# A transformer block in float32: the MLP's first product as a 2x2 block product in seven multiplications

## The chip, the core and the metric

The kernel runs on one core of one Trainium2 chip. The metric is the time on the device of one execution in microseconds, as the median of several runs. The shape is fixed: 512 tokens, model width 1024, an MLP of 4096 hidden columns, all in float32.

## The reference, cut to what matters

The block mixes the tokens (a gated linear attention and a latent attention, merged by gates), projects the result back, and applies an MLP with a squared ReLU between two norms:

```python
h = x
h = h + merged @ w_out            # merged: the token mixing, 512 x 1024
m = rmsnorm(h, g_mlp)             # 512 x 1024
h = h + square(relu(m @ w_ff1)) @ w_ff2     # w_ff1: 1024 x 4096, w_ff2: 4096 x 1024
out = rmsnorm(h, g_final)
```

The result has to be of float32 precision. The change concerns the line with `w_ff1` and `w_ff2`, and the end of the line before it, beside which the MLP begins.

## The kernel before

**Precision.** TensorE multiplies a rounded float32 type. So every operand is split into a high part (a rounded copy, ScalarE, L93) and a low part (the rest, `src - hi`, VectorE, L94), and one product is three matmuls (`mm3`, L88 to L90: high by high, high by low, low by high). Whatever is multiplied has to go through a split first. `halves` is a pool of four pairs of high and low tiles for weights.

**The MLP before.** The hidden columns are done in four quarters (`qd`) of 1024. Each quarter has two parts, called f and g after their tiles.
In f, `hidden` forms 128 hidden columns for all tokens (`proj_begin` loads and splits the weights, `proj_run` multiplies): 8 steps over the model width, three matmuls each, 512 tokens wide, accumulated in the PSUM bank `f`. There are eight such products a quarter. `pair_units` takes the ReLU and the square (ScalarE) and makes the seven left operands that g needs: `left_sums` adds and subtracts the token halves and column halves (VectorE), and `split_first`, `split_sum` and `split_corner` split them.
In g, the quarter's hidden tile (512 x 1024) is multiplied with 1024 rows of `w_ff2` as a 2x2 block product by a scheme with seven multiplications instead of eight. Blocks are 256 tokens by 512 columns on the left and 512 by 512 on the right. The weight blocks are called B11, B12, B21, B22, and B11 is overwritten by sums and differences of them (`add_w2`, VectorE, L1000, 1024 elements wide). `ORDER` gives the sequence of the seven: 1, 5, 6, 3, 7, 4, 2. One multiplication (`block_product`) is 24 matmuls, 512 wide, for each of two row blocks. Its weights are made ready two products ahead (`prep`). The results are gathered in PSUM (`gx`, `gz`, `gw`) and added to the residual rows by `add_rows` (L1488, VectorE).

**The part before the MLP.** The product with `w_out` runs in seven multiplications as well (`wo_product`). `flipped` transposes the normed rows, two blocks of 128 tokens at a time for each token half, and `Flipped.evacuate` scales and splits the transposed rows from PSUM into `mT`, the operand of all f products. The first two f products (`early`) are begun beside the end of the product with `w_out`.

**What sets the order.** The code lists the operations, and a scheduler then orders them on each engine by estimated times, except where an order is written out: `in_program_order` fixes the order of the code on TensorE, VectorE and ScalarE up to the beginning of quarter 0, and on GpSimd up to there too; `goes_behind` moves single operations on named engines. Each engine takes its own instructions strictly in order and waits at each for its operands. Plain loads are issued by SyncE (SP); transfers that add to the tile they land in are issued by GpSimd. `stage` is a pool of three tiles (tag `wf`) for weights that are loaded. [...]

## Time and profile before

| | |
|---|---|
| median of 3 runs | 751.37 us (750.8 to 751.4) |
| span of the profiled execution | 749.5 us |
| TensorE busy | 740.9 us, 3698 matmuls |
| VectorE busy | 589.9 us, 853 operations |
| ScalarE busy | 461.8 us, 789 operations |
| GpSimd busy | 173.3 us, 244 operations |
| moved to and from the chip's memory | 83.25 MB read, 2.10 MB written |

The profile is one execution, taken on the core by the hardware profiler. PE is TensorE, PEld its weight load, DVE VectorE, ACT ScalarE, POOL GpSimd, SP SyncE. A row of the trace has the start in us, the duration, the engine, the line of the code, the operation, the tiles written and read, and the shapes; a bracket at its end tells how long the engine had been idle and what it waited for. The chain of waits follows the work that ended last back from the last instruction, and shares the span out by engine. The MLP takes from about 412 us to the end: quarter 0 to 512, then a quarter each 82 us, and the last one up to 749.

### The profile page before, as it was taken

The numbers are of one execution on the slowest core, as the hardware profiler recorded it, in microseconds if no ns is written. First come the engines' busy times: TensorE is split into PE (matmuls) and PEld (weight loads), VectorE is DVE, ScalarE is ACT, GpSimd is POOL, SyncE is SP. The second block draws the span as 40 slices with busy tenths as digits, with TensorE's granted clock in tenths as the row PEclk, the third lists the DMA queues.
The fourth block names the chain that finished last, engine by engine and source line by source line (L and its number), as shares of the span: only waits on it lengthen the run. The fifth ranks groups of instructions, "written<-read, shape, count | busy, mean of one in ns | idle before, by whom it ended". The sixth has DMA issues, their size and how long they took to land.

```text
span 749.5 us, 10256 instructions
## 1 busy us (share of the span) xinstructions
PE 740.9 (99%) x3698; PEld 628.1 (84%) x3698; DVE 589.9 (79%) x853; ACT 461.8 (62%) x789; POOL 173.3 (23%) x244
## 2 busy tenths in 40 slices
PE   9999999999999999999999999999999999999996
PEld 7888888888889888899988988888888888888885
DVE  7777887989988787888898788857697578747785
ACT  7556574686686576887956765436643464445644
POOL 0732010252663732256741100000000000000023
PEclk9999999999999999999999999999999999999999
DMA  9849682611321234459797410551136310640003
GB/s 311 265 113 228 193 176 84 103 40 29 84 57 33 46 89 106 110 143 254 196 240 230 121 56 28 169 172 53 57 101 182 112 57 27 196 143 0 29 0 113
DMA packets 94723, 88.90 MB, mean 119 GB/s; under 512 B 15793, under 2 KB 66993, under 8 KB 94673
## 3 DMA queue, kind: packets, MB, share of 16 engines
q1 hardware_dynamic: 88176, 75.64, 34.1%
q0 software_dynamic: 6208, 12.32, 9.3%
q8 instruction: 29, 0.48, 0.3%
q10 hardware_dynamic: 288, 0.28, 0.1%
q14 instruction: 22, 0.17, 0.1%
HBM read 83.25 MB, written 2.10 MB: 114 GB/s over the span
## 4 chain that ended last, share of the span: by engine, by line
PE 98%; issue 0%; DVE 0%; POOL 0%; ACT 0%; POOLq 0%
PE f L89 8%; PE f L88 8%; PE f L90 8%; PE gx L88 4%; PE gx L89 4%; PE gx L90 4%; PE first L330 3%; PE gz L88 2%; PE gz L89 2%; PE tp L1145 2%; PE gz L90 2%; PE zb L88 1%; PE zb L89 1%; PE zb L90 1%; PE av L89 1%; PE av L90 1%
## 5 line engine op out<-in xcount | busy, mean ns | idle before, releaser
L1750 POOL DMA_DIRECT2D gfin<-in_g_final x1 | 0.6, 629 | 283.4 <-PE f L90 283.4
L1000 DVE TENSOR_TENSOR w<-w,w 128x1024 f32<-128x1024 f32 x32 | 38.8, 1222 | 0.3
L1125 DVE TENSOR_REDUCE top<-s 128x1 f32<-128x512 f32 x32 | 21.6, 683 | 4.9 <-PE s L90 4.8
L1130 ACT ACTIVATE e<-s,top 128x512 f32<-128x512 f32 x32 | 22.0, 687 | 3.5 <-DVE top L1125 2.5
L94 DVE TENSOR_TENSOR pT<-tp,pT 128x512 fp32r<-128x512 f32 x32 | 21.8, 683 | 2.4 <-ACT pT L93 2.0
L1488 DVE TENSOR_TENSOR h<-h,gx 128x512 f32<-128x512 f32 x32 | 21.5, 683 | 1.9 <-PE gx L90 1.8
L93 ACT ACTIVATE pT<-tp 128x512 fp32r<-128x512 f32 x32 | 19.0, 595 | 3.2 <-PE tp L1145 3.2
L1145 PE MATMUL tp<-ident,e 128*128 128x128 f32 x128 | 19.4, 274 | 0.0
L88 PE MATMUL av<-pT,v 128*128 128x256 f32 x64 | 19.1, 299 | 0.0
L93 ACT ACTIVATE ghb<-y 128x512 fp32r<-128x512 f32 x16 | 10.1, 633 | 14.0 <-DVE y L946 14.0
L1554 ACT ACTIVATE fa<-f 128x512 f32<-128x512 f32 x32 | 18.5, 579 | 0.0
L90 PE MATMUL av<-pT,v 128*128 128x256 f32 x64 | 18.2, 285 | 0.0
L89 PE MATMUL av<-pT,v 128*128 128x256 f32 x64 | 18.2, 284 | 0.0
L1145 PEld LDWEIGHTS tp<-ident,e 128*128 128x128 f32 x128 | 15.2, 140 | 3.1 <-ACT e L1136 0.7
L94 POOL TENSOR_TENSOR qF<-qk,qF 128x512 fp32r<-128x512 f32 x4 | 6.6, 1642 | 37.6 <-ACT qF L93 37.6
L93 ACT ACTIVATE b_00h<-w 128x1024 fp32r<-128x1024 f32 x7 | 7.4, 1060 | 12.6 <-PE gx L90 6.0
L93 ACT ACTIVATE b_10h<-w 128x1024 fp32r<-128x1024 f32 x7 | 7.4, 1059 | 12.1 <-PE gz L90 6.0
L93 ACT ACTIVATE b_20h<-w 128x1024 fp32r<-128x1024 f32 x7 | 7.4, 1059 | 12.1 <-PE gz L90 6.0
L88 PE MATMUL s<-kbuf,q 96*128 96x512 f32 x32 | 14.1, 439 | 0.0
L1563 ACT ACTIVATE px<-fa 128x256 f32<-128x256 f32 x32 | 13.4, 418 | 1.0
L671 POOL DMA_DIRECT2D gvw<-in_w_in x4 | 4.8, 1226 | 38.7 <-DVE gvw L676 34.0
L996 POOL DMA_DIRECT2D w<-in_w_out x10 | 12.3, 1402 | 6.5 <-DVE bo60l L94 5.3
(1802 smaller groups left out, 2950.5 us busy)
## 6 DMA issues: line engine op xcount, KB each, us to landing
w<-in_w_ff SPq DMA_DIRECT2D x64, 256.0 KB, 3.6
w<-in_w_out POOLq DMA_DIRECT2D x10, 512.0 KB, 8.5
grw<-in_w_in SPq DMA_DIRECT2D x8, 512.0 KB, 9.3
zaw<-in_w_in SPq DMA_DIRECT2D x8, 512.0 KB, 8.0
gvw<-in_w_in SPq DMA_DIRECT2D x8, 512.0 KB, 4.9
w<-in_w_out SPq DMA_DIRECT2D x16, 256.0 KB, 5.6
x<-in_xt SPq DMA_DIRECT2D x8, 256.0 KB, 5.1
vw<-in_w_first SPq DMA_DIRECT2D x8, 256.0 KB, 5.3
```

The lines of the kernel that those rows point to most:

```text
L88: nc.tensor.matmul(acc, lh, rh, start=start, stop=False, skip_group_check=onto)
L89: nc.tensor.matmul(acc, lh, rl, start=False, stop=False, skip_group_check=onto)
L90: nc.tensor.matmul(acc, ll, rh, start=False, stop=stop, skip_group_check=onto)
L93: nc.scalar.activation(hi, src, AF.Copy)
L94: rest.tensor_tensor(lo, src, raw(hi), op=ALU.subtract)
L330: nc.tensor.matmul(f_accs[i], a[:, i * P : (i + 1) * P], b, start=k == 0 and x == 0, stop=k == KD - 1 and x == 2)
L1000: nc.vector.tensor_tensor(wq[dst][g], wq[x][g], wq[y][g], op=op)
L1125: nc.vector.tensor_reduce(top, acc, axis=AX.X, op=ALU.max, negate=True)
L1130: nc.scalar.activation(e, acc, AF.Exp, bias=top, accum_out=tot[:, qt % 2 : qt % 2 + 1])
L1145: nc.tensor.transpose(tp[:, k * P : (k + 1) * P], e[:, k * P : (k + 1) * P], ident)
L1488: nc.vector.tensor_tensor(hc, hc, acc, op=op)
L1554: nc.scalar.activation(a, acc, AF.Relu)
```

## The change

The f part of each quarter is multiplied by seven as well. The left operand is the normed input `m` in blocks of 256 tokens by 512 columns, and the right one is a 1024 x 1024 piece of `w_ff1` in blocks of 512. So one f product is now 48 matmuls, all 256 tokens wide, and there are seven a quarter instead of eight of 24 that are 512 wide.

- The left operands of f are the same for all quarters and are made once, in quarter 0, from the transposed rows in PSUM (`m_upper`, `m_lower`, `m_sum`, `m_split`). The sums of the upper half (`m_upper_raw`) and two of the others are made on GpSimd. `mT` and `Flipped.evacuate` are gone (`fm.block` hands out the bank instead).
- A class `Mlp` holds one part (f or g) of one quarter, and `phases` lists the eight in turn. The sequence of products is `SEVEN` = 1, 2, 5, 6, 3, 7, 4, and `ORDER` = 1, 5, 6, 3, 7, 4, 2 for the last g.
- Weights: a part loads its blocks with `load` (SP), and forms the sums in place. Behind the split for product 1, GpSimd adds B12 to B11 (two operations of 1024) and issues a transfer that adds B22 onto B12 (`onto`). Before product 6, VectorE adds B22 to B11, and behind it GpSimd issues a transfer that adds B21 onto B11.
- `keep` moves the results of f out of PSUM, `left_sums` forms g's left operands in place: one difference on VectorE, the other three sums (six operations of 512) on GpSimd, where before all were on VectorE. `split_left` splits them, and those of products 6, 3 and 7 only at the beginning of g.
- Every part prepares its weights two products ahead, across the border between parts. The order of the code is held on TensorE, VectorE and ScalarE through the first products of quarter 0.

The diff, cut (where removed lines are left out, the functions above show them):

```diff
...
+        def block(self, half, k):
+            c = (k // 4) * 256
+            return self.banks[half][k % 4][:, c : c + 256], self.gains[:, k : k + 1]
...
-    def add_w2(dst, x, y, op):
-        for g in range(NP // 2):
-            nc.vector.tensor_tensor(wq[dst][g], wq[x][g], wq[y][g], op=op)
...
+    m_left, m_raw = {}, {}
+    def m_upper():
+        for m in (1, 2):
+            m_left[m] = quarter(f"mh{m}"), quarter(f"ml{m}")
+        for k in range(KD):
+            hi, lo = m_left[1 + k // NP]
+            src, gain = fm.block(0, k)
+            split_scaled(hi[:, k % NP], lo[:, k % NP], src, gain)
+    def m_upper_raw():
+        for m in (1, 2):
+            hi, lo = m_left[m]
+            m_raw[m] = pair_tiles(f"mr{m}")
+            for b, dst in enumerate(m_raw[m]):
+                c = slice(2 * b, 2 * b + 2)
+                nc.gpsimd.tensor_tensor(dst, raw(hi[:, c]), raw(lo[:, c]), op=ALU.add)
+    def m_split(m):
+        m_left[m] = hi, lo = quarter(f"mh{m}"), quarter(f"ml{m}")
+        for b, s in enumerate(m_raw[m]):
+            c = slice(2 * b, 2 * b + 2)
+            split(hi[:, c], lo[:, c], s)
+    def m_lower():
+        a22, s1 = pair_tiles("mr4"), pair_tiles("mr5")
+        m_raw[4], m_raw[5] = a22, s1
+        for b in range(2):
+            for i in range(2):
+                src, gain = fm.block(1, NP + 2 * b + i)
+                nc.scalar.activation(a22[b][:, i], src, AF.Copy, scale=gain)
+                src, gain = fm.block(1, 2 * b + i)
+                nc.vector.scalar_tensor_tensor(s1[b][:, i], src, gain, a22[b][:, i], op0=ALU.mult, op1=ALU.subtract)
+        m_split(5)
+    def m_lower_raw():
+        m_raw[0] = a21 = pair_tiles("mr0")
+        for k in range(NP):
+            src, gain = fm.block(1, k)
+            nc.scalar.activation(a21[k // 2][:, k % 2], src, AF.Copy, scale=gain)
+    def m_sum(m, x, y, op, eng=nc.gpsimd):
+        m_raw[m] = pair_tiles(f"mr{m}")
+        for dst, a, b in zip(m_raw[m], m_raw[x], m_raw[y]):
+            eng.tensor_tensor(dst, a, b, op=op)
...
+    class Mlp:
+        def __init__(self, n):
+            self.n, self.qd, self.second = n, n // 2, n % 2 == 1
+            self.name = f"{'g' if self.second else 'f'}{self.qd}"
+            self.order = ORDER if n == 2 * NQ - 1 else SEVEN
+            self.right, self.left, self.accs = {}, {}, {}
+        def source(self, x, g):
+            w, r, c = (w2, self.qd * D, 0) if self.second else (w1, 0, self.qd * D)
+            r += (x // 2) * S + g * 2 * P
+            c += (x % 2) * S
+            return w[r : r + 2 * P, c : c + S].rearrange("(k p) w -> p k w", p=P)
+        def tiles(self, x):
+            if x == B22:
+                if x not in ring:
+                    ring[x] = [stage(2, S, f"w22{g}") for g in range(2)]
+                return ring[x]
+            return wq[{B11: B21 if self.second else B11, B21: B22, B12: B12}[x]]
+        def load(self, x):
+            for g, dst in enumerate(self.tiles(x)):
+                nc.sync.dma_start(dst, self.source(x, g))
+        def onto(self, dst, x):
+            for g, d in enumerate(self.tiles(dst)):
+                nc.gpsimd.dma_start(d, self.source(x, g), accum_op=ALU.add)
+        def add(self, dst, x, eng, gs=range(2)):
+            for g in gs:
+                a, b = self.tiles(dst)[g], self.tiles(x)[g]
+                eng.tensor_tensor(a, a, b, op=ALU.add)
+        def split_right(self, m, g, late=False):
+            wh, wl = halves(2, S, f"{self.name}{m}{g}")
+            src = self.tiles({2: B21, 3: B22, 7: B12}.get(m, B11))[g]
+            nc.scalar.activation(wh, src, AF.Copy)
+            self.right.setdefault(m, []).append((wh, wl))
+            def lows():
+                nc.vector.tensor_tensor(wl, src, raw(wh), op=ALU.subtract)
+            return lows if late else lows()
+        def behind(self, m):
+            after_ = phases[self.n + 1 : self.n + 3]
+            if m == 1:
+                self.add(B11, B12, nc.gpsimd)
+                self.onto(B12, B22)
+            elif m == 6:
+                self.onto(B11, B21)
+            elif m == 4:
+                if len(after_) == 2:
+                    after_[1].load(B11)
+            elif m in (2, 3, 7) and after_:
+                after_[0].load({2: B21, 3: B22, 7: B12}[m])
+        def prepare(self, m):
+            if m == 6:
+                self.add(B11, B22, nc.vector)
+            for g in range(2):
+                self.split_right(m, g)
+            self.behind(m)
+        def banks(self, m):
+            if m in (1, 2, 5):
+                tag = {1: "at" if self.second else "mm", 2: "mm", 5: "at"}[m]
+                self.accs[m] = [ps(tag, f"{self.name}{'xwz'[m // 2]}{b}") for b in range(2)]
+            return self.accs[{2: 2, 5: 5, 3: 5}.get(m, 1)]
+        def first(self, m, by_rows=False):
+            accs = self.banks(m)
+            right = self.right.pop(m)
+            lh, ll = m_left[m]
+            steps_ = [(b, i, p) for b in range(2) for i in range(2) for p in range(NP)]
+            if by_rows:
+                steps_.sort(key=lambda x: x[2])
+            for b, i, p in steps_:
+                wh, wl = right[p // 2]
+                c = slice((2 * b + i) * P, (2 * b + i + 1) * P)
+                mm3(accs[b][:, i * HT : (i + 1) * HT], wh[:, p % 2, c], wl[:, p % 2, c], lh[:, p], ll[:, p],
+                    m in (1, 2, 5) and p == 0 and i == 0, p == NP - 1, True)
+        def keep(self, m):
+            accs = self.accs[{2: 2, 5: 5, 3: 5}.get(m, 1)]
+            c = {1: 1, 2: 1, 5: 4, 6: 2, 3: 2, 7: 4, 4: 0}[m]
+            if m in (1, 5, 6, 4):
+                self.left[c] = pair_tiles(f"{self.name}a{c}")
+            for d, acc in zip(self.left[c], accs):
+                acc = acc.rearrange("p (a b) -> p a b", a=2)
+                if m in (1, 5, 6):
+                    nc.scalar.activation(d, acc, AF.Copy, scale=-1.0 if m == 6 else 1.0)
+                    continue
+                if m == 4:
+                    nc.scalar.activation(d, acc, AF.Relu)
+                else:
+                    nc.vector.tensor_tensor(d, d, acc, op=ALU.subtract if m == 7 else ALU.add)
+                    nc.scalar.activation(d, d, AF.Relu)
+                nc.scalar.activation(d, d, AF.Square)
+            if m in (2, 3, 7):
+                self.split_left(c)
+        def split_left(self, m, lows=None):
+            highs = pair_tiles(f"{self.name}h{m}", F32R)
+            lows = lows or pair_tiles(f"{self.name}l{m}", F32R)
+            for s, hi, lo in zip(self.left[m], highs, lows):
+                split(hi, lo, s)
+            self.left[m, "hl"] = highs, lows
+        def left_sums(self):
+            a11, a12, a21, a22 = (self.left[x] for x in (1, 2, 0, 4))
+            def sums(eng, dst, a, b, op):
+                for d, x, y in zip(dst, a, b):
+                    eng.tensor_tensor(d, x, y, op=op)
+            sums(nc.vector, a22, a21, a22, ALU.subtract)
+            low = tl([P, 2, 2, HT], F32R, "wf", 3, f"{self.name}l5")
+            self.left[5] = a22
+            self.split_left(5, [low[:, b] for b in range(2)])
+            sums(nc.gpsimd, a21, a11, a21, ALU.subtract)
+            sums(nc.gpsimd, a11, a22, a11, ALU.subtract)
+            sums(nc.gpsimd, a12, a12, a11, ALU.add)
+            self.left[6], self.left[3], self.left[7] = a11, a12, a21
+        def second_product(self, m, accs, begin, rb, cols=slice(0, S), out_cols=slice(0, S)):
+            highs, lows = phases[self.n - 1].left[m, "hl"]
+            for p in range(NP):
+                c = slice(rb * P, (rb + 1) * P)
+                lh, ll = (x[p // 2][:, p % 2, c] for x in (highs, lows))
+                wh, wl = self.right[m][p // 2]
+                mm3(accs[rb][:, out_cols], lh, ll, wh[:, p % 2, cols], wl[:, p % 2, cols],
+                    begin and p == 0, p == NP - 1, not begin)
...
+    phases = []
+    phases += [Mlp(n) for n in range(2 * NQ)]
+    f0 = phases[0]
...
-    load_w2(0, B21)
+    phases[1].load(B11)
     flipped(0)
-    at = traced()
-    early = [proj_begin(w1, 0, "f00", "mm")]
-    goes_behind((at, traced()), span["sums"], SP_ONLY)
+    f0.split_right(1, 0)
     first_half_square(2, 1)
...
-    fm.evacuate(0)
+    m_upper()
     first_half_square(3, 1)
...
+    f0.add(B11, B12, nc.gpsimd, (0,))
+    lows = f0.split_right(1, 1, True)
     wo_product(4, (0,))
     add_rows(2, 0, xs_[0])
     second_half_square(2, 0)
     wo_product(4, (1,))
-    at = traced()
     add_rows(3, 0, xs_[1])
     rs2 = row_rstd(hparts[2])
     second_half_square(3, 0)
...
     rs3 = row_rstd(hparts[3])
     scaled(2, rs2)
     scaled(3, rs3)
-    span["norm", 3] = at, traced()
-    proj_run(early[0], mT, 0)
-    proj_run(early[1], mT, 0, range(5))
+    for g in range(2):
+        f0.split_right(2, g)
+    f0.behind(2)
+    f0.add(B11, B12, nc.vector, (1,))
+    m_upper_raw()
+    f0.onto(B12, B22)
+    f0.first(1, True)
     flipped(2)
     flipped(3)
...
+    f0.first(2)
+    m_lower()
+    f0.split_right(5, 0)
+    m_sum(6, 5, 1, ALU.subtract, nc.vector)
+    m_lower_raw()
+    f0.split_right(5, 1)
+    m_split(6)
+    m_sum(7, 1, 0, ALU.subtract)
+    m_sum(3, 2, 6, ALU.add)
+    f0.keep(1)
+    f0.prepare(6)
+    f0.first(5, True)
+    f0.keep(2)
+    f0.keep(5)
+    m_split(3)
+    f0.prepare(3)
+    f0.first(6)
     in_program_order(begun, PE_ONLY + SPLITTERS)
     in_program_order(attending, (mybir.EngineType.Pool,))
...
+    f0.prepare(7)
+    f0.keep(6)
+    m_split(7)
+    m_split(4)
+    steps = [(ph, m) for ph in phases for m in ph.order]
+    for n, (ph, m) in enumerate(steps):
+        if n < 4:
+            continue
+        last = ph is phases[-1]
+        ahead, behind = None, False
+        if n + 2 < len(steps):
+            ahead = steps[n + 2]
+            behind = last and ahead[1] == 2
+            if not behind:
+                ahead[0].prepare(ahead[1])
+        if not ph.second:
+            ph.first(m)
+            ph.keep(m)
+            if m == 4:
+                ph.left_sums()
+            continue
+        f_ph = phases[ph.n - 1]
+        at = ph.order.index(m)
+        if last and at == 0:
             gfin = u4("gfin", F32, (P, D))
             nc.gpsimd.dma_start(gfin, t["g_final"].partition_broadcast(P))
...
+        if at < 3:
+            f_ph.split_left((6, 3, 7)[at])
+        if m == 4 and last:
+            last_rows(ph, ph.banks(4))
+            break
+        accs = ph.banks(m)
+        adding = traced()
+        for rb in range(2):
+            ph.second_product(m, accs, m in (1, 2, 5), rb)
+            upper, lower = rb, 2 + rb
+            if m in (1, 2):
+                add_rows(upper, 0, accs[rb])
+            elif m in (6, 3):
+                add_rows(upper, 1, accs[rb], ALU.subtract if m == 6 else ALU.add)
+            elif m in (5, 7):
+                add_rows(lower, 1, accs[rb], ALU.subtract if m == 7 else ALU.add)
             else:
...
+                add_rows(lower, 0, accs[rb])
+            if last and m in (3, 7):
+                out_first(upper if m == 3 else lower)
+        if behind:
+            added = traced()
+            ahead[0].prepare(ahead[1])
+            goes_behind((added, traced()), (adding, added), SPLITTERS[1:])
...
```

178 lines of the change are left out of this document (24 added, 154 removed).

## Prediction

> **What bounds the kernel now.** I read the totals and the chain of waits on the page first, then the matmuls in order of time, then the stretches of the MLP.
>
> ```profile
> span 749.5 us, 10256 instructions
> PE 740.9 (99%) x3698; PEld 628.1 (84%) x3698; DVE 589.9 (79%) x853; ACT 461.8 (62%) x789; POOL 173.3 (23%) x244
> PE 98%; issue 0%; DVE 0%; POOL 0%; ACT 0%; POOLq 0%
> 461.00:512.00 51.00, 51.00 (x225) 42.22 (x226) 36.23 (x46) 21.98 (x28) 0.00 (x0) 1.00 0.47 139
> 699.48 0.63 POOL L1750 DMA_DIRECT2D gfin<-in_g_final  x1 [283.40 <-PE f L90]
> ```
>
> TensorE carries 98% of the chain and is busy 99% of the span; every other engine has room. The fourth line is one stretch of the MLP (columns: time, then busy us of TensorE, weight load, VectorE, ScalarE, GpSimd, granted clock, DMA share, GB/s): VectorE 36 of 51 us, GpSimd nothing. The last row says that GpSimd rests 283 us before it, so through the MLP. A saving of TensorE time is therefore a saving of the whole, for as long as the other engines hand over in time. The times of the runs have a median of 751.4 us; the span of the profiled execution is 749.5, so about 1.9 us lie around it. I sum against the span and add 1.9.
>
> **The matmuls.** The price of both widths stands in the trace, in the same place and with a new stationary operand each time.
>
> ```profile
> 412.13 0.28 PE L88 MATMUL f<-mT,f00h 128*128 128x256 f32 x1
> 415.00 0.28 PE L88 MATMUL f<-mT,f01h 128*128 128x256 f32 x1
> ...
> 430.88 0.39 PE L88 MATMUL f<-mT,f03h 128*128 128x512 f32 x1
> 452.64 0.39 PE L88 MATMUL f<-mT,f07h 128*128 128x512 f32 x1
> ```
>
> The first two rows are 24 matmuls apart, 2.87 us: 0.1196 us for 256 tokens. The other two are 96 apart, 21.76 us: 0.2267 for 512. Before, the first product is 96 narrow and 720 wide matmuls: 11.5 + 163.2 = 174.7 us. After it is 4 quarters of 7 products of 48 narrow ones, 1344 x 0.1196 = 160.7. The second product keeps its 672 wide ones. TensorE saves 14.0 us, 3.3 to 3.5 a quarter. [...]
>
> One f product now takes 48 x 0.1196 = 5.74 us, one g product 24 x 0.2267 = 5.44.
>
> **What the other engines get.** Durations from start to start:
>
> ```profile
> 710.10 1.22 DVE L94 TENSOR_TENSOR b_30l<-w,b_30h 128x1024 fp32r<-128x1024 f32 x1
> 711.24 0.69 DVE L94 TENSOR_TENSOR glc<-z,ghc 128x512 fp32r<-128x512 f32 x1
> 711.84 1.22 DVE L94 TENSOR_TENSOR b_31l<-w,b_31h 128x1024 fp32r<-128x1024 f32 x1
> ...
> 404.01 1.05 ACT L93 ACTIVATE bo40h<-w 128x1024 fp32r<-128x1024 f32 x1
> 404.96 1.04 ACT L93 ACTIVATE bo41h<-w 128x1024 fp32r<-128x1024 f32 x1
> ...
> 591.41 0.62 ACT L93 ACTIVATE ga<-px 128x512 fp32r<-128x512 f32 x1
> 591.93 0.41 ACT L93 ACTIVATE gd<-qx 128x256 fp32r<-128x256 f32 x1
> 593.27 0.63 ACT L93 ACTIVATE ghb<-y 128x512 fp32r<-128x512 f32 x1 [0.94 <-DVE y L946]
> ```
>
> VectorE: 1.14 us for 1024 wide, 0.60 for 512. ScalarE: 0.95, and 0.52 to 0.63 for 512. A quarter now has on VectorE 28 splits and 4 weight sums of 1024 (36.5 us) and 36 operations of 512 (21.6): 58 of the 78.3 us that TensorE would need. ScalarE has 28 copies and some 36 operations of 512, about 47. Neither is a bound by its total. The weights become 16 plain transfers of 512 KB and 8 accumulating ones, 12 MB, 153 GB/s over 78.3 us, about what the quoted stretch moves at a DMA share of 0.47.
>
> GpSimd gets four weight sums of 1024 and six left sums of 512 a quarter. Its price, and what it does to VectorE:
>
> ```profile
> 34.57 0.75 POOL L638 TENSOR_TENSOR xz<-x 128x256 f32<-128x256 f32 x1
> 35.03 1.37 DVE L94 TENSOR_TENSOR gr10l<-grw,gr10h 128x1024 fp32r<-128x1024 f32 x1 [1.08 <-ACT gr10h L93]
> 35.28 1.72 POOL L639 TENSOR_TENSOR xz<-x,xy 128x256 f32<-128x256 f32 x1
> 36.33 1.75 DVE L94 TENSOR_TENSOR gr11l<-grw,gr11h 128x1024 fp32r<-128x1024 f32 x1
> 36.96 1.72 POOL L638 TENSOR_TENSOR xz<-x 128x256 f32<-128x256 f32 x1
> ...
> 727.17 1.29 POOL L1591 TENSOR_TENSOR ms<-h,gfin 128x512 f32<-128x512 f32 x1
> 727.55 1.99 DVE L94 TENSOR_TENSOR b_31l<-w,b_31h 128x1024 fp32r<-128x1024 f32 x1
> 733.63 1.21 DVE L94 TENSOR_TENSOR b_31l<-w,b_31h 128x1024 fp32r<-128x1024 f32 x1
> 733.84 2.16 POOL L1591 TENSOR_TENSOR ms<-h,gfin 128x512 f32<-128x512 f32 x1
> 734.76 0.68 DVE L1488 TENSOR_TENSOR h<-h,gx 128x512 f32<-128x512 f32 x1
> ...
> 136.04 2.44 POOL L671 DMA_DIRECT2D gvw<-in_w_in  x2 [34.02 <-DVE gvw L676]
> 136.71 1.22 DVE L94 TENSOR_TENSOR gv50l<-gvw,gv50h 128x1024 fp32r<-128x1024 f32 x1
> ```
>
> A GpSimd sum of 256 takes 0.75 us alone, of 512 1.29; 1024 is not shown. It lies between 1.29 (no dearer than 512) and 3.4 (twice the longest row here at 256, 1.72); the step of 0.54 per 256 gives 2.4, which I take. Where two operations on SBUF meet, the later one waits for the earlier: at 727.55 VectorE takes 1.99 in place of 1.22, at 733.84 GpSimd 2.16 in place of 1.29, and from 34.57 to 38.6 they go strictly in turn. An operation that reads PSUM (734.76) is not held, and issuing a transfer (136.04, 1.2 us each) holds nobody. So sums moved to GpSimd take VectorE's time for operations on SBUF all the same, and at 1.29 for 0.60. [...]
>
> **Where it lies on the path.** The f stages have slack: their two GpSimd sums precede product 5, with product 2 (5.74 us) between. The change from f to g has none. Let T be the end of f's product 4 in quarter 2, so g's products 1, 2, 5, 6 should start at T, T+5.44, T+10.88, T+16.32. The split buffers of g's product 1 come free with f's product 7, at T-5.74; behind them stand one sum from PSUM (0.60) and the first split (1.14), so the first GpSimd weight sum can start at T-3.9. In the changed kernel's order, what must then be done up to the second weight split of g's product 6 is, on VectorE, 9 operations of 1024 (the other splits of products 1, 2, 5, 6 and the two sums with B22) and 9 of 512 on SBUF: 10.3 + 5.4 = 15.7 us. On GpSimd it is both weight sums and all six left sums, because ScalarE's queue has the left splits that wait for those sums ahead of the weight copy: 4.8 + 7.7 = 12.5. In turn that is 28.2 us, to T+24.3. TensorE wants this tile at its eighth matmul of product 6, T+16.32+1.6 = T+17.9. It waits 6.4 us, part of it already in product 5. Quarter 1 has one 512 more: 7.0. Quarter 3: 6.4. Quarter 4 goes 1, 5, 6, so product 6 comes at T+10.88, and it needs both halves of its left sums: VectorE 12.8, GpSimd 11.3, to T+20.2, wanted at T+12.7: 7.5. Together 27.3 us. The floor of these terms is nothing (no operations meet), the ceiling with 3.4 us for a sum of 1024 is 8 x 1.0 more.
>
> Quarter 1 also has a head that is issued in written order. Between the first matmul of product 6 and that of product 3 stand f061's low split (1.14), a PSUM sum (0.60), ten ScalarE operations of 512 (5.5), a weight copy (0.95) and its low split (1.14): 9.4 us against 5.74. That is 3.7 late, whatever GpSimd does.
>
> ```profile
> 414.03 2.05 POOL L184 TENSOR_TENSOR hp<-hp,mhalf 128x1 f32<-128x1 f32 x2 [1.88 <-DVE hp L181]
> ...
> 417.00 1.75 PE mb L199 x16
> ...
> w<-in_w_out POOLq DMA_DIRECT2D x10, 512.0 KB, 8.5
> ```
>
> The first row is two small powers that hold GpSimd until 416.1. Then its eight sums of 512 (10.3) stand against VectorE's 8 operations of 1024 and 6 of 512 on SBUF (12.7) until product 6 has its low split: to 439.1. Product 6 should begin at 412.1 + 3 x 5.74 + 1.75 for the transposes (second row) = 431.1, so up to 8.0 more. The head costs 3.7 to 11.7; only two of the eight sums are needed early, so I take the middle, 7.7.
>
> Sum: 749.5 - 14.0 + 27.3 + 7.7 = 770.5 span, 772.4 us as timed. Accumulating transfers (third row: 8.5 us from issue to landing at 512 KB) have three products of cover and I cost them at nothing; without it, see the third rival.
>
> **Rivals.**
> First, faster: the sums meet VectorE in its idle time. For it speaks VectorE's idle share of a quarter, 20 of 78 us, and that GpSimd is idle in the MLP now; against it that the 28.2 us above must fit between T-3.9 and T+17.9, 21.8 us. It decides if less than about 6 us of GpSimd's 12.5 collide. Then only the head's 3.7 and about 2 at the last change are left: 751.4 - 14.0 + 5.7 = 743.
>
> Second, half of the collisions are hidden and the head costs its floor: 751.4 - 14.0 + 13.6 + 3.7 = 755. For it: product 5's wait and product 6's overlap with PSUM operations that are not held. Against: they are already left out of my count.
>
> Third, the transfer onto B11 is late too. In g it is issued only after product 6's splits, T+24.3; two issues and 8.5 us later, T+35.2, product 4's copy may begin, and product 4 starts at T+32.6+6.4 = T+39.0. Copy and two low splits take 3.2 us, so 0.6 us is spare; 3 us more of landing would cost about 2.4 a quarter: 782. The 8.5 speaks against it, being a median under load.
>
> **Chances.** Mine 0.62 (own range 762 to 782), the first rival 0.21, the second 0.09, the third 0.08. The range goes from 741 to 782. What this kernel's runs can tell from no change is about 0.2%, 1.5 us. Faster 0.22 (first rival and a little of the second), same 0.02, slower 0.76.
>
> **What would show it.** Each step right: narrow matmuls 0.12 us apart; in g's products 5 and 6 TensorE idle 6 to 7 us a quarter, released by VectorE's low splits; GpSimd left sums above 1.29 us and VectorE splits above 1.22 between T-4 and T+24; f stages of quarters 2 to 4 at 40.2 us without idle time; a gap of 3 to 4 us before f0's product 3. The prediction is wrong if GpSimd's left sums run at 1.29 while VectorE's splits keep 1.22, if narrow matmuls in long runs are dearer than 0.12, or if TensorE waits for something not in this list, such as PSUM banks or a transfer.

## The result and the profile after

The changed kernel takes 788.05 us (786.5 to 788.6), the kernel before beside it 751.38: a ratio of 1.0487, 95% interval 1.0472 to 1.0502. The forecast was slower, 772 us, in a range of 741 to 782; the direction is right and the time is 6 us outside the range. One execution of a later run (both edits together, below), the one that was profiled, took 2290 us where the other three took 772 to 775, and is left out of that run's time.

From the page of the changed kernel: the span, the busy times, the granted clock in 40 slices, and the chain of waits by engine. The last line is the clock row of the kernel before.

```profile
span 786.6 us, 11492 instructions
PE 746.1 (95%) x4226; PEld 650.0 (83%) x4226; DVE 664.6 (84%) x830; ACT 496.3 (63%) x807; POOL 309.3 (39%) x323
PEclk9999999999999999999999899999989999999898
PE 72%; DVE 18%; issue 6%; ACT 3%; POOL 1%; DVEq 0%; POOLq 0%; ACTq 0%
...
PEclk9999999999999999999999999999999999999999
```

TensorE has 528 more matmuls and is busy 5 us longer, though it should have saved 14. The clock row shows part of why: 9 in all slices before, it is 8 in four slices of the MLP now. The chain that was 98% TensorE has 18% on VectorE.

The same kernel by stages: f of quarter 1 (with the transposes), g of quarter 1, f and g of quarter 2, g of quarter 4 to the end. Columns: time, busy us of TensorE, weight load, VectorE, ScalarE, GpSimd, then granted clock, DMA share, GB/s.

```profile
412.50:469.20 56.70, 47.32 (x354) 45.46 (x353) 48.99 (x51) 38.19 (x63) 26.32 (x17) 0.94 0.46 112
469.20:515.80 46.60, 41.02 (x171) 32.30 (x170) 44.39 (x43) 22.10 (x28) 22.18 (x14) 0.96 0.53 136
515.80:556.10 40.30, 40.30 (x337) 40.30 (x336) 30.18 (x28) 28.03 (x40) 9.14 (x6) 1.00 0.65 157
556.10:602.80 46.70, 42.30 (x170) 32.88 (x169) 44.38 (x42) 20.11 (x25) 21.85 (x14) 0.93 0.54 135
730.20:786.60 56.40, 41.99 (x181) 33.19 (x180) 46.02 (x50) 25.67 (x44) 29.69 (x23) 0.90 0.33 75
```

By matmuls and transposes alone these stages should take 41.9, 38.1, 40.2, 38.1 and (as before) 45.7 us. The f stage of quarter 2 is there, with no idle time. Every g is 8.5 us or more over, and quarter 1's f 14.8. In the g stages of quarters 1 to 3 VectorE is busy 44.4 of some 46.7 us, the time included for which GpSimd holds it up; in quarter 4, which has the end of the kernel in it, 46.0 of 56.4.

What TensorE waited for, the longest first (total us, times, longest):

```profile
PE g3z L90 <- DVE f3l L94: 4.3, 2, 3.3
PE f0z L90 <- DVE f051l L1586: 2.5, 1, 2.5
PE g0z L89 <- DVE g051l L1586: 2.5, 1, 2.5
PE g2z L89 <- DVE g250l L1586: 2.1, 1, 2.1
PE g1z L89 <- DVE g150l L1586: 2.1, 1, 2.1
PE g3x L88 <- DVE h L1465: 1.8, 1, 1.8
...
PE g1z L88 <- DVE h L1465: 0.8, 1, 0.8
```

The largest are of the kind that the prediction names, for low splits in g's product 5 and in the head. Another kind it doesn't name: VectorE's read (`h`, L1465) of an earlier product in the same PSUM banks, 0.8 to 1.0 us before g's product 3 in quarters 1 to 3, and 1.8 us before product 6 in quarter 4.

The change from f to g in quarter 2, on VectorE, GpSimd and ScalarE (by matmuls alone g would start product 5 at 567.0):

```profile
552.46 3.31 POOL L1577 TENSOR_TENSOR w<-w,w 128x1024 f32<-128x1024 f32 x1 [20.32 <-DVE g110l L1586]
553.42 6.83 DVE L94 TENSOR_TENSOR f1l<-f1a,f1h 128x512 fp32r<-128x512 f32 x2
556.84 2.85 POOL L1577 TENSOR_TENSOR w<-w,w 128x1024 f32<-128x1024 f32 x1
560.77 1.21 DVE L1586 TENSOR_TENSOR g120l<-w,g120h 128x1024 fp32r<-128x1024 f32 x1
561.00 6.06 POOL L1664 TENSOR_TENSOR f1a<-f1a,f1a 128x512 f32<-128x512 f32 x3
561.91 2.31 DVE L1586 TENSOR_TENSOR g121l<-w,g121h 128x1024 fp32r<-128x1024 f32 x1
564.14 1.78 DVE L94 TENSOR_TENSOR f1l<-f1a,f1h 128x512 fp32r<-128x512 f32 x1
565.84 1.77 DVE L1664 TENSOR_TENSOR f1a<-f1a,f1a 128x512 f32<-128x512 f32 x1
567.65 0.64 ACT L93 ACTIVATE f1h<-f1a 128x512 fp32r<-128x512 f32 x1 [5.61 <-DVE f1a L1664]
567.76 5.18 POOL L1664 TENSOR_TENSOR f1a<-f1a,f1a 128x512 f32<-128x512 f32 x3 [0.69 <-DVE f1a L1664]
568.19 1.04 ACT L1582 ACTIVATE g150h<-w 128x1024 fp32r<-128x1024 f32 x1
569.51 2.29 DVE L1586 TENSOR_TENSOR g150l<-w,g150h 128x1024 fp32r<-128x1024 f32 x1
```

GpSimd's weight sum takes 3.31 us against VectorE's splits, and two VectorE operations of 512 take 6.83 together in place of 1.3. The three left sums behind 561.00 take 2 us each, and in turn with them g121l needs 2.31 and the left splits 1.77. That holds back the second left difference (565.84), the ScalarE split that needs it (567.65, which had ScalarE idle for 5.6 us), and with it the weight copy for product 5 in the same queue (568.19) and its low split (569.51).

Behind the wait stands a second loss. TensorE's matmuls there:

```profile
568.03 0.39 PE L90 MATMUL g1w<-g121h,f1l 128*128 128x512 f32 x1
569.28 0.51 PE L88 MATMUL g1z<-g150h,f1h 128*128 128x512 f32 x1 [0.86 <-ACT g150h L1582]
571.85 0.79 PE L89 MATMUL g1z<-g150l,f1h 128*128 128x512 f32 x1 [2.07 <-DVE g150l L1586]
572.45 0.63 PE L90 MATMUL g1z<-g150h,f1l 128*128 128x512 f32 x1
572.87 0.63 PE L88 MATMUL g1z<-g150h,f1h 128*128 128x512 f32 x1
...
577.40 0.44 PE L89 MATMUL g1z<-g150l,f1h 128*128 128x512 f32 x1
577.67 0.40 PE L90 MATMUL g1z<-g150h,f1l 128*128 128x512 f32 x1
```

Product 5 waits 0.86 us, gets one matmul, and waits 2.07. The next 12 distances, up to 577.4, are 0.42 to 0.60 us (nine of them 0.42 or 0.43) in place of 0.2267. For each stage I took the starts of neighbouring matmuls in order of time and counted what a distance exceeds 0.1196 or 0.2267 us: excesses over 0.45 us as waits, smaller ones over 0.05 as half speed.

| stage | waits, us | half speed, us | forecast waits, us |
|---|---|---|---|
| f, quarter 1 | 10.8 | 3.9 | 7.7 |
| g, quarter 1 | 6.3 | 2.1 | 7.0 |
| g, quarter 2 | 5.1 | 3.4 | 6.4 |
| g, quarter 3 | 6.5 | 2.0 | 6.4 |
| g, quarter 4 | 8.2 | 2.8 | 7.5 |
| sum | 36.9 | 14.1 | 35.0 |

Saved 14.0, lost 36.9 + 14.1: 37.0 us. The spans differ by 37.1.

### The profile page after: what moved, and what is told of

It reads as the page before. It is cut to its first block, busy times and chain, and to the rows that moved or that the text cites. A ratio compares the mean times of both kernels' runs of the same rounds, so it can differ in the third digit from the quotient of the medians.

```text
span 786.6 us, 11492 instructions
## 1 busy us (share of the span) xinstructions
PE 746.1 (95%) x4226; PEld 650.0 (83%) x4226; DVE 664.6 (84%) x830; ACT 496.3 (63%) x807; POOL 309.3 (39%) x323
## 4 chain that ended last, share of the span: by engine, by line
PE 72%; DVE 18%; issue 6%; ACT 3%; POOL 1%; DVEq 0%; POOLq 0%; ACTq 0%
PE first L326 3%; DVE h L1465 2%; PE tp L1122 2%; DVE w L1577 2%; PE zb L88 1%; PE zb L90 1%; PE zb L89 1%; DVE f0l L94 1%; DVE f1l L94 1%; DVE f2l L94 1%; PE av L89 1%; PE av L88 1%; PE av L90 1%; DVE f3l L94 1%; PE s L88 1%
## 5 line engine op out<-in xcount | busy, mean ns | idle before, releaser
L1577 POOL TENSOR_TENSOR w<-w,w 128x1024 f32<-128x1024 f32 x15 | 41.9, 2793 | 131.2 <-DVE g010l L1586 22.3
L1572 POOL DMA_DIRECT2D w<-in_w_ff x32 | 38.8, 1224 | 59.1 <-DVE f260l L1586 10.1
L94 DVE TENSOR_TENSOR f2l<-f2a,f2h 128x512 fp32r<-128x512 f32 x14 | 17.7, 1276 | 3.0 <-ACT f2h L93 2.8
L94 DVE TENSOR_TENSOR f1l<-f1a,f1h 128x512 fp32r<-128x512 f32 x14 | 17.7, 1276 | 3.0 <-ACT f1h L93 2.8
L94 DVE TENSOR_TENSOR f3l<-f3a,f3h 128x512 fp32r<-128x512 f32 x14 | 17.1, 1230 | 2.8 <-ACT f3h L93 2.8
L90 PE MATMUL av<-pT,v 128*128 128x256 f32 x64 | 18.2, 284 | 0.0
L667 POOL DMA_DIRECT2D zaw<-in_w_in x4 | 4.8, 1215 | 32.7 <-DVE zaw L672 28.0
L94 DVE TENSOR_TENSOR f0l<-f0a,f0h 128x512 fp32r<-128x512 f32 x14 | 13.1, 950 | 3.7 <-ACT f0h L93 3.7
L1153 POOL TENSOR_TENSOR mx<-tb,yg 128x256 f32<-128x256 f32 x8 | 7.7, 967 | 19.8 <-DVE tb L1150 13.8
L93 ACT ACTIVATE f0h<-f0a 128x512 fp32r<-128x512 f32 x14 | 8.5, 620 | 9.2 <-POOL f0a L1664 6.8
L88 PE MATMUL s<-kbuf,q 96*128 96x512 f32 x32 | 14.1, 439 | 0.0
```

Of the source, the lines that this page charges most:

```text
L88: nc.tensor.matmul(acc, lh, rh, start=start, stop=False, skip_group_check=onto)
L90: nc.tensor.matmul(acc, ll, rh, start=False, stop=stop, skip_group_check=onto)
L93: nc.scalar.activation(hi, src, AF.Copy)
L94: rest.tensor_tensor(lo, src, raw(hi), op=ALU.subtract)
L1572: nc.gpsimd.dma_start(d, self.source(x, g), accum_op=ALU.add)
L1577: eng.tensor_tensor(a, a, b, op=ALU.add)
```

## The experiments

Two theories at first. In turn: VectorE's operations on SBUF and GpSimd's sums go one after the other (the split g121l above took 2.31 us in place of 1.21), and TensorE pays for it twice, by the wait and by half speed (0.42 to 0.60 us a matmul in place of 0.2267). Queue order: it is the places in VectorE's and ScalarE's queues that make product 5 late, whatever GpSimd does. All times are medians, ratios are against the kernel before on the same chip.

### Taking the sums off GpSimd

Left sums to VectorE (778.9 us, 1.0374, 1.0358 to 1.0389):

```diff
-            sums(nc.gpsimd, a21, a11, a21, ALU.subtract)
+            sums(nc.vector, a21, a11, a21, ALU.subtract)
...
```

> The six left sums of each quarter go back from GpSimd to VectorE; the weight sums stay on GpSimd. In-turn theory (VectorE's operations on SBUF and GpSimd's sums exclude each other, and TensorE loses twice, by the wait and by half speed behind it): GpSimd's 7.7 us leave the change from f to g and VectorE gets 3.6, so the waits shrink by 4 us a quarter and most of the 2 to 3 us at half speed go with them: g stages of 46.7 become about 40.5, total 760 to 770 us. Queue-order theory (what delays product 5 is the place of the second a22 difference behind weight splits in VectorE's and ScalarE's queues, GpSimd's speed is beside the point): VectorE has 3.6 us more and nothing is gained, 788 to 800.

B11 + B12 to VectorE (775.1 us, 1.0319, 1.0304 to 1.0335):

```diff
-                self.add(B11, B12, nc.gpsimd)
+                self.add(B11, B12, nc.vector)
```

> The sums B11 + B12 of all stages behind f0 go from GpSimd to VectorE; the left sums stay on GpSimd. In-turn theory: 4.8 us of GpSimd against 2.3 of VectorE, the waits in g shrink by about 2.5 us and a little of the half speed goes: 3 to 4 us a quarter, 770 to 778 us in all; the f stages stay at 40.3. Queue-order theory: 786 to 797.

B11 + B12 by an accumulating transfer (775.7 us, 1.0344, 1.0321 to 1.0367):

```diff
-                self.add(B11, B12, nc.gpsimd)
+                self.onto(B11, B12)
```

> The sums B11 + B12 of all stages behind f0 are made by an accumulating transfer in place of two GpSimd operations; GpSimd issues 2 more transfers a stage, the left sums stay on GpSimd. In-turn theory: 4.8 us leave the change from f to g and nothing comes to VectorE, the waits in g shrink from about 5.3 to 1 or 2 us and the half speed goes: 6 to 7 us a quarter, 758 to 766 us, if the transfers (6 us from issue to landing in this kernel) land in time, as 2 x 1.2 + 6 us after product 1's splits they should. Transfer theory (the sums by transfer land later than GpSimd's did, and product 5 waits for them): waits for a transfer in product 5 of f and g, 785 to 800. Queue-order theory: 786 to 790.

The first and the third edit together (773.0 us, 1.0301, 1.0280 to 1.0322). Its stages can't be read from its profile.

> Both edits: B11 + B12 by transfer, left sums on VectorE; GpSimd does no sums behind quarter 1's head. In-turn theory: on VectorE 19 us are left for 21.8, so only the 1 us before product 3 stays in each g: g stages 39 to 40 us, total 752 to 760 us; what is left over the old kernel is the head, 14.7 us against the 14.0 that TensorE saves. Queue-order theory: 788 to 800. If it comes below 751 the head must have moved too.

Each gains, 9, 13, 12 and 15 us, where the queue-order theory expected nothing. But only the second came where the in-turn theory put it, the others 9 to 13 us above their ranges, and two edits that gain 9 and 12 us alone gain 15 together.

Moving an operation to another engine also lets the scheduler order the queues anew, and in the first two runs VectorE's and ScalarE's orders did change. In the run with transfers they did not: TensorE's matmuls stand in the order of the changed kernel to the end, VectorE's and ScalarE's operations up to the last change from f to g. There quarter 2's g fell from 46.7 to 42.3 us with the two weight sums gone from GpSimd and nothing else reordered, so GpSimd's sums cost time in one and the same order, and the queue-order theory alone falls. Quarter 2's g in that run:

```profile
552.50:594.90 42.40, 39.39 (x171) 31.31 (x170) 37.89 (x40) 20.03 (x25) 17.98 (x12) 1.00 0.72 175
```

What is left there? ScalarE's weight copies,

```profile
562.75 1.06 ACT L1582 ACTIVATE g151h<-w 128x1024 fp32r<-128x1024 f32 x1 [1.01 <-DMA w<-in_w_ff]
...
569.11 1.06 ACT L1582 ACTIVATE g160h<-w 128x1024 fp32r<-128x1024 f32 x1 [4.25 <-DVE w L1577]
```

wait 1.0 us for the transfer (g151h) and 4.25 us for VectorE's sum B11 + B22 (g160h), which stands in VectorE's queue behind all of product 5's splits. So a second cause is left, the order of that queue or the amount of work in it; the order could be tried.

### The head, and the speed behind a wait

On top of both edits, the head's eight sums to VectorE as well, each where it is needed (770.5 us, 1.0246, 1.0213 to 1.0279):

```diff
-                nc.gpsimd.tensor_tensor(dst, raw(hi[:, c]), raw(lo[:, c]), op=ALU.add)
+                nc.vector.tensor_tensor(dst, raw(hi[:, c]), raw(lo[:, c]), op=ALU.add)
...
-    def m_sum(m, x, y, op, eng=nc.gpsimd):
+    def m_sum(m, x, y, op, eng=nc.vector):
...
+    m_upper_raw(1)
     m_sum(6, 5, 1, ALU.subtract, nc.vector)
...
     f0.prepare(6)
+    m_upper_raw(2)
+    m_sum(3, 2, 6, ALU.add)
```

> The kernel with B11 + B12 by transfer and the left sums on VectorE, and in quarter 1's head the eight sums of 512 moved from GpSimd to VectorE too, each where its result is first needed (two ahead of product 6's left operand, the others behind product 6's weights). In-turn theory: VectorE reaches the low splits of product 5 at about 430 us and of product 6 at 433.5 in place of 433 and 440, the head's waits shrink from 10.8 us to 4 or 5 and its half speed from 3.9 to at most 2: quarter 1's f in 47 to 50 us in place of 56.7, 8 us less than the run with both edits alone (774), so 763 to 768. Queue-order theory: VectorE has 4.8 us more to do in the head, no gain, 773 to 780. What the g stages still wait for will be seen in this trace: for a split that stands behind others in VectorE's queue (order), or for a transfer (landing).

Quarter 1's f fell from 56.7 to 53.0 us, not to 47 to 50. Products 5 and 6 were as early as expected (waits of 2.9 us in all up to there), but 3.8 us were now lost before product 3, the place and size that the prediction gives for ScalarE's written order "whatever GpSimd does"; in the changed kernel itself only 2.0 us of it show, where product 6 is later.

The speed by itself: trains of 60 matmuls with waits of chosen length between them.

```diff
+        for i in range(TRAIN):
+            nc.tensor.matmul(acc, left, src, start=i == 0, stop=i == TRAIN - 1)
+        nc.scalar.activation(keep, acc, AF.Copy)
+        for _ in range(copies):
+            nc.scalar.activation(keep, keep, AF.Copy)
+        nc.scalar.activation(right[(n + 1) % 2], keep, AF.Copy, scale=1.0 / 700)
```

> A kernel of its own that computes nothing of the reference: 45 trains of 60 matmuls (512 wide, about 13.6 us), and between two trains a wait on a chain of 2 to 10 ScalarE operations of 512, so about 1 to 5.5 us. If it is the single wait that sets the speed behind it: trains behind waits under about 2 us keep 0.227 us a matmul, those behind waits over 3.5 us begin at 0.43 for 3 to 6 us, and between the two it depends on the moment. If half speed in the changed kernel came from something else (transfers, GpSimd), no train here runs at 0.43 whatever its wait.

One row is a train: start, duration, and in brackets the wait before it.

```profile
22.58 13.89 PE L43 MATMUL acc<-right,left 128*128 128x512 f32 x60 [1.35 <-ACT right L47]
39.20 13.90 PE L43 MATMUL acc<-right,left 128*128 128x512 f32 x60 [2.74 <-ACT right L47]
118.87 15.51 PE L43 MATMUL acc<-right,left 128*128 128x512 f32 x60 [2.07 <-ACT right L47]
214.52 15.51 PE L43 MATMUL acc<-right,left 128*128 128x512 f32 x60 [2.73 <-ACT right L47]
137.77 16.50 PE L43 MATMUL acc<-right,left 128*128 128x512 f32 x60 [3.39 <-ACT right L47]
234.08 16.15 PE L43 MATMUL acc<-right,left 128*128 128x512 f32 x60 [4.05 <-ACT right L47]
```

A train takes 13.89 us at full speed. Behind waits of 1.35 to 1.41 us it always does. Behind 2.07 us it always takes 1.6 us more. Behind 2.73 or 2.74 us it once lost nothing (39.20) and 1.6 us every other time; longer waits cost 1.4 to 2.6, with no order by length. The clock that was granted shows why (columns: time, then busy us of TensorE, weight load, ScalarE, GpSimd, granted clock, DMA share, GB/s):

```profile
116.00:119.41 3.41, 1.34 (x6) 0.83 (x5) 1.85 (x3) 0.00 (x0) 1.00 0.00 0
119.41:122.82 3.41, 3.41 (x9) 2.63 (x8) 0.00 (x0) 0.00 (x0) 0.50 0.00 0
```

In this trace the clock changes only on a beat of 3.41 us, and behind a wait it stays at half for one or two beats; in the changed kernel's trace the stretches at 0.50 behind waits last 3.41 or 6.83 us. The wait of 2.07 us (116.80 to 118.87) lies within one beat, and the next runs at 0.50. The wait of 2.74 us that cost nothing lies across two, with 1.03 us in one and 1.71 in the other. The sequence of waits repeats every 177.5 us, which is 52 beats, so the repeats of a wait meet the same moment and count as one case, not as five. A wait's price thus has a second part, up to 1.7 us (half of 3.41) for each beat at half clock behind it, and no transfer or GpSimd is needed for it: GpSimd and DMA stand at 0.00 in both rows.

### The order of the products and of the queues

In f of quarters 2 to 4 product 3 goes last, so that all of g's left operands but a12's can be made beside it (772.2 us, 1.0279, 1.0251 to 1.0307):

```diff
-            self.order = ORDER if n == 2 * NQ - 1 else SEVEN
+            self.order = ORDER if n == 2 * NQ - 1 else SEVEN if self.second or n == 0 else (1, 2, 5, 6, 7, 4, 3)
...
-            sums(nc.vector, a12, a12, a11, ALU.add)
...
+        def left_last(self):
+            for d, x, y in zip(self.left[3], self.left[3], self.left[6]):
+                nc.vector.tensor_tensor(d, x, y, op=ALU.add)
...
```

> The run before (no GpSimd sums, quarter 1's head on VectorE; 770 us) with one thing changed: in quarters 2 to 4 the products of f go 1, 2, 5, 6, 7, 4, 3 in place of 1, 2, 5, 6, 3, 7, 4, so that all but two of g's left operands can be formed and split beside f's last product (5.74 us), and only a12 and the sum with it come behind it. If what is left of the waits at the change from f to g comes from the left operands all hanging on f's last product: g of quarters 2 and 3 in about 39 us in place of 42 to 43, and g of quarter 4 (which wants product 5's left operand second) in 47 to 50 in place of 54.4; 756 to 761 us in all. If it comes from the weights' chain on VectorE alone (B11 + B22 and the splits of product 6), quarters 2 and 3 stay at 42 to 43 and only quarter 4 gains: 764 to 768. The new risk: product 4's transfer has one product less to land in; if it is late, f stages grow over 40.3 us with waits for product 4's split.

g of quarters 2 and 3 went from 42.3 and 43.0 us to 39.5 and 39.4, as expected, and that of quarter 4 from 54.4 to 51.9, but f of quarters 2 to 4 grew from 40.3, 40.3 and 41.2 to 43.4, 44.5 and 45.5: the risk came true in another form. ScalarE in quarter 2's f:

```profile
531.78 1.06 ACT L1582 ACTIVATE f140h<-w 128x1024 fp32r<-128x1024 f32 x1 [1.04 <-PE f1x L90]
535.36 1.06 ACT L1582 ACTIVATE f141h<-w 128x1024 fp32r<-128x1024 f32 x1 [2.52 <-DMA w<-in_w_ff]
536.32 0.58 ACT L1640 ACTIVATE f1a<-f1x 128x512 f32<-128x512 f32 x1
```

The weight copy f141h waits 2.52 us for the transfer onto B11; behind it in the queue stands the second copy of product 6 out of PSUM (536.32), and product 7, which adds to the same banks, waits for that copy. The gain moved into a new wait.

The same with product 3's operands ahead in the head (771.4 us, 1.0261, 1.0228 to 1.0294):

```diff
+    m_split(3)
     f0.first(5, True)
+    f0.prepare(3)
-    f0.keep(2)
     f0.keep(5)
-    m_split(3)
-    f0.prepare(3)
+    f0.keep(2)
```

> As the run sent with it, and in quarter 1's head product 3's left split and weights are put ahead of the copies of products 2 and 5 in the written order of ScalarE and VectorE. The prediction put 3.7 us there whatever GpSimd does; the head without GpSimd's sums waits 3.8 us at just that place (2.96 for ScalarE's weight copy, 0.52 for the low split, and their starts) with half speed behind it. If that order is the cause: quarter 1's f goes from 53 to 47 or 48 us, 5 to 6 us less than the run sent with it, 750 to 756. If it is the amount of work: within 2 us of it.

The wait before product 3 went from 3.0 to 0.4 us, and one of 4.6 came before product 7. Quarter 1's f took 54.3 us, 1.3 more.

Then the new waits of those two runs taken away: product 6's copies ahead of product 4's weights, B11 + B12 on GpSimd in f and on VectorE in the last g, product 7's left split earlier in the head (757.0 us, 1.0080, 1.0063 to 1.0096):

```diff
+                if not self.second:
+                    self.add(B11, B12, nc.gpsimd)
+                elif self.n == 2 * NQ - 1:
+                    self.add(B11, B12, nc.vector)
+                else:
+                    self.onto(B11, B12)
...
+            if copied_first:
+                kept = traced()
+                ahead[0].prepare(ahead[1])
+                goes_behind((kept, traced()), (at, kept), SPLITTERS[:1])
```

> The order 1, 2, 5, 6, 7, 4, 3 for f in quarters 2 to 4 with the new waits of that run taken away: the copies of product 6 stand ahead of product 4's weight copies on ScalarE (it waited 2.5 us there for the transfer onto B11), B11 + B12 goes back to GpSimd in the f stages, where it never showed, and to VectorE in the last g, where the transfer came 3 us late; and in the head the left split of product 7 stands ahead of the copies of product 2. In-turn theory with the order of the queues as its second part: f of quarters 2 to 4 in 40.3 us again, g of quarters 2 and 3 in 39.5, g of quarter 4 in 48 to 50, quarter 1's f in 47 to 49 and its g in 42: a span of 749 to 753 and 751 to 755 us, no clear difference to the kernel before. If the waits only move on, as they did in the last two runs: 760 to 770.

Its stages: f and g of quarter 1, f and g of quarter 2, g of quarter 4.

```profile
412.10:466.60 54.50, 46.96 (x354) 45.54 (x353) 46.39 (x63) 40.68 (x66) 14.04 (x11) 0.91 0.62 139
466.60:505.80 39.20, 38.29 (x169) 31.41 (x169) 37.00 (x45) 19.73 (x25) 6.24 (x5) 1.00 0.59 157
505.80:546.20 40.40, 40.40 (x338) 40.36 (x338) 30.23 (x32) 26.42 (x38) 10.68 (x8) 1.00 0.80 186
546.20:585.90 39.70, 38.72 (x170) 31.37 (x170) 36.64 (x44) 21.16 (x27) 6.38 (x5) 1.00 0.59 156
706.20:755.30 49.10, 39.55 (x182) 31.94 (x180) 39.91 (x56) 26.60 (x47) 14.68 (x16) 0.95 0.37 86
```

The f of quarters 2 to 4 and the g of quarters 1 to 3 are now within 1.6 us of the matmuls alone, and quarter 4's g within 3.4. Several edits were made at once, so which of them gained how much is not shown, and the time is 2 us above the range expected. Most of what is left sits in quarter 1's f: 54.5 us against 41.9, with one wait of 5.05 us before product 7.

Two more runs start from this better order: one varies the order in quarter 1's head (759.4 us, 1.0111, 1.0094 to 1.0128), and the other is the same with the left sums on GpSimd again (767.0 us, 1.0219, 1.0200 to 1.0238).

```diff
+    f0.keep(6)
+    at = traced()
+    f0.prepare(7)
+    weights_7 = at, traced()
     in_program_order(begun, PE_ONLY + SPLITTERS)
...
-    f0.prepare(7)
-    f0.keep(6)
...
+            if n == 4:
+                for x in range(at, traced()):
+                    goes_behind((x, x + 1), weights_7, SPLITTERS[1:])
```

> The run before (757 us) with the last long wait of its head taken out: product 7 of quarter 1's f waited 5.05 us for ScalarE's copy of product 6, which stood behind product 4's weight copies; here the copies of product 6 and the weights of product 7 are in the written order ahead of them. If the order of ScalarE's queue was the cause: the 5.2 us and most of the 4.5 at half speed behind it go, quarter 1's f in 46 to 48 us, span 746 to 749 and 748 to 751 us, level with the kernel before or a little under it. If the wait moves on to the transfer onto B11 for product 4 (issued behind product 6's splits at about 436, 6 to 8.5 us to land, wanted at 447): 751 to 755.

```diff
-            sums(nc.vector, a21, a11, a21, ALU.subtract)
+            sums(nc.gpsimd, a21, a11, a21, ALU.subtract)
...
```

> The run sent with it, with the six left sums of each quarter put back on GpSimd and nothing else changed: it asks what GpSimd's sums cost once the queues are in a better order. In-turn theory: 7.7 us of GpSimd against VectorE's 3.6 at the change from f to g in all four quarters; quarters 2 and 3 have most of f's last product (5.74 us) for it and lose 0 to 2 us, quarter 1 (old order) 2 to 4, quarter 4 (product 5's operands second) 3 to 5, half speed behind the longer waits: 5 to 12 us slower than the run sent with it. Queue-order theory alone (GpSimd's sums never mattered): within 2 us of it.

The varied head gained nothing: a wait of 3.6 us came back at the same place, now for product 7's weight copy behind product 2's copies. Moving the sums back costs 7.5 us, inside the range of the in-turn theory (5.0 by the two profiled executions: 1.5 or 1.6 us in each of the four g stages, less 0.4 in quarter 1's f and 0.8 before it). Quarter 2's g without and with GpSimd's left sums:

```profile
548.40:588.20 39.80, 38.80 (x171) 31.43 (x170) 36.72 (x45) 21.25 (x27) 6.37 (x5) 1.00 0.59 157
```

```profile
548.70:590.10 41.40, 38.98 (x170) 31.26 (x169) 39.10 (x43) 22.23 (x28) 14.31 (x10) 1.00 0.59 153
```

GpSimd is busy 8 us longer and VectorE 2.4 us longer, although VectorE has six operations of 512 a quarter fewer in this kernel. Some weight splits and PSUM reads changed places on VectorE too, so the 7.5 us are those of the sums together with the order that they bring.

### Quarter 1: the wait that moves

The long wait of quarter 1 was then taken from each place where it stood. Product 2's copies behind product 6's (756.9 us, 1.0076, 1.0063 to 1.0090):

```diff
+    f0.add(B11, B22, nc.vector)
     m_split(6)
...
-    f0.keep(2)
     f0.first(6)
     f0.keep(6)
...
     f0.prepare(7)
...
+    f0.keep(2)
```

> As the run before without GpSimd's left sums, with the copies of product 2 of quarter 1's f (two VectorE sums and six ScalarE operations, which still stood ahead of product 6's copies and product 7's weights) moved behind them, and product 6's weight sums one place forward. If the order of the queues is what is left in the head: the 3.8 us before product 7 and 2 to 3 us at half speed go, quarter 1's f from 53.7 to 47 to 49 us and its g stays at 40 to 42: 751 to 755 us. If the amount of work on VectorE is: quarter 1's f stays over 52 us and the wait moves to product 4.

TensorE in written order past the end of that f, up to g's second product (758.5 us, 1.0100, 1.0087 to 1.0114):

```diff
+        if n == 9:
+            in_program_order(begun, PE_ONLY)
```

> The run before (757 us) with one thing changed: TensorE's matmuls keep the written order up to the end of quarter 1's f. In that run the scheduler had put the first matmuls of g (whose low split came 2.2 us late) ahead of the end of f's product 4. If the rest of quarter 1's loss (93.3 us for f and g where the matmuls and transposes need 80) comes from the order: 3 to 5 us off, 752 to 754. If VectorE's amount of work there sets it: the wait moves to another place and the time stays within 2 us, 755 to 758.

The last change from f to g in order as well (756.8 us, 1.0075, 1.0062 to 1.0089):

```diff
+            if self.n == 2 * NQ - 2:
+                self.split_left(6)
...
+                            issued_after(i, reads[1].name)
```

> As the run sent with it, and at the last change from f to g the reads of product 3's PSUM banks go ahead of the weight splits of g's product 5 on VectorE, and product 6's left operand is split one product earlier. The two waits there (0.9 us for the PSUM read, 1.8 us for the low left split) and 0.7 to 2.1 us at half speed should go: 3 to 5 us less than the run sent with it, 748 to 751, level with the kernel before. If it stays over 753, the sevenfold f product cannot be fed on these engines by order alone.

And the reads of product 7 ahead of g's first weight splits (759.6 us, 1.0111, 1.0095 to 1.0128):

```diff
-    f0.keep(2)
+    f0.keep(2, False)
...
+                if n == 5:
+                    ph.split_left(1)
+                    ph.keep(3)
+                    ph.split_left(4)
```

> As the last run (757 us), with the one long wait of quarter 1 taken out: product 4 of its f waited 5.7 us for VectorE's read of product 7 in the same PSUM banks, which stood behind the first weight splits of g; here the two reads stand ahead of those splits, and the left splits of products 1 to 3's results behind the reads. If the order is the cause: 5 us of wait and 3 at half speed go, quarter 1's f from 55 to 47 or 48 us; what was moved back costs g at most 2: 748 to 752 us, level with the kernel before. If VectorE's work between product 6 and g (it is busy without a break there) is the cause, the wait comes back at g's first products: over 754.

The last run's quarter 1, f and g:

```profile
411.70:459.20 47.50, 44.13 (x353) 42.48 (x352) 42.88 (x57) 36.58 (x60) 12.87 (x11) 1.00 0.61 141
459.20:505.70 46.50, 39.88 (x170) 31.08 (x169) 40.54 (x50) 23.75 (x31) 7.45 (x6) 1.00 0.59 151
```

f came to 47.5 us as expected, and g went from 38.9 to 46.5. f and g of quarter 1 together take 93.6, 93.7, 93.3, 94.2, 94.0 and 94.0 us in the six runs of order (the head's first reordering, the combined one, and these four; 95.6 with the varied head), whether the long wait stands before product 7 or 4 or in g; the matmuls and transposes need 80.0. So among these orders the loss only moves. All four runs came out above the times expected if the order were the cause (748 to 755 us). VectorE is busy 83.4 of the 94.0 us; that its amount of work is the bound is the reading that fits, but no run took work away from it there, so it isn't shown. In g of quarter 4 the waits of 0.9 and 1.8 us became 1.2 and two of 0.6, next to nothing in sum. The stage fell from 50.7 to 49.1 us, but by half clock: it was 49.1 in the combined run with the old waits, and 50.6 in the last run with the new ones. That the order helped there isn't shown. No version came under the kernel before; the best are 0.75% over it.

## Why the prediction was right or wrong

**The matmuls: right.** The narrow ones stand 0.12 us apart in long runs, f stages of quarters 2 to 4 take 40.3 us against 40.2 forecast, and the account closes with 14.0 saved.

**The waits in g: near in sum, partly by luck.** 27.3 us were forecast, 26.1 measured. The mechanism named is at work: sums of 1024 on GpSimd took 2.38 us at best (2.4 estimated), the six left sums 1.72 to 2.08 in the median of a quarter (1.29 alone), and VectorE's splits were stretched between them (2.31 us for g121l in place of 1.21). But most of the wait fell in product 5, not 6. And 5.3 of the 26.1 us are waits for PSUM banks, which were not in the list and which the prediction gave as a sign of being wrong; another 1.5 fall in product 2. Without these 19.3 are left of the 27.3, so that the two sums agree is partly luck. Moving the sums shows how much hangs on GpSimd: 9 to 15 us of the whole, and 7.5 in the better order. The forecast of these runs put all of the g stages' loss on it and was too high: with no sums left on GpSimd in g, and VectorE doing the left sums, the four g stages still waited 18.2 us, now behind a VectorE queue that is late by its order or its amount of work.

**The head: within its bounds, above the value taken.** 10.8 us of waits; 3.7 to 11.7 were given and 7.7 taken. 8.9 us fell before products 1, 2, 5 and 6 (up to 8.0 forecast), but 2.9 of them stayed when GpSimd's sums were gone. The written order's part showed with 2.0 of 3.7 before product 3, and with all of it once GpSimd's sums were gone. The middle was 3.1 us too low.

**The failed step: "Sum: 749.5 - 14.0 + 27.3 + 7.7".** It prices a wait at its length. TensorE ran at half speed behind the waits, 14.1 us over five stages, and that term is missing; with it and the head's 3.1 us more, less 1.2 in g, the sum gives 786.5 against a span of 786.6. That the sum closes is bookkeeping; that a wait by itself brings half clock is what the trains show (0.50 behind 2.07 us). The kernel before, with a clock of 1.00 all through the MLP's f and g, has no row for it. With some 2 us for each of the five stages with waits, which the trains showed afterwards, the forecast would have been about 782, and the stages lost 2.0 to 3.9 each.

**The rivals.** The first (the sums fall in VectorE's idle time, 743) is refuted by the stretched rows, and the second (half of the waits, 755) by 26.1 us in g against its 13.6 and 10.8 in the head against its 3.7. The third (the transfer onto B11 late) did not happen in the changed kernel, where TensorE never waits for it; it came in f in the run that put product 4 one place earlier, 2.5 us as soon as its slack was taken.

## What to carry to other kernels

A wait of TensorE cost its length here and, where enough of one 3.41 us beat was idle (1.84 us or more was enough each time), up to 1.7 us more for each beat at half clock behind it. So a kernel with TensorE at 99% can lose more by waits than a few per cent of its matmuls are worth: here 14 us were saved, and 37 us of waits brought another 14 at half clock. Work moved to GpSimd was not free where VectorE's queue was full of splits and sums on SBUF (2.31 us for a split that took 1.21 alone): look for the stretch where both queues are full, not at the engine's share of the whole. And when a scheme makes all operands of the next stage hang on the last product of this one, choose the order of the products so that the last one feeds the fewest; by itself that took 2.5 to 3.6 us off the g of quarters 2 to 4 here, and the new waits that it made in f cost more until they were taken away.

## What the runs showed of the hardware that was not expected

How much of one beat of 3.41 us passes without a matmul told better here than the length of a wait whether the next beat ran at half clock. In the traces of all runs but that of both edits together, for beats at full clock: one with 1.84 us or more idle was followed by one at half clock each time (83 of 83, 39 of them in the trains), one with less than 1.3 us never, and in between both happened (in the changed kernel 1.64 and 1.72 us were followed by half clock, 1.31 to 1.45 us were not). So waits close together added up: in the changed kernel 0.86 and 2.07 us with one matmul between them were followed by 5.5 us at 0.42 to 0.60 us a matmul. And one wait had two prices: 2.4 us before product 7 of quarter 2's f cost no half clock in the first run with product 3 last, and 1.4 us in the next, where 1.9 us of it in place of 1.6 fell into one beat.
